# A transformer block on one core: the table of times is carried on through the second output product into the MLP, 81 pieces are shifted singly, and ScalarE makes both copies of the turned attention weights

## The chip, the cores and the metric

One core of one Trainium2 chip runs the whole kernel. The core has four engines that work at the same time, each through its own queue in order: TensorE (PE, matmuls), VectorE (DVE), ScalarE (ACT) and GpSimd (POOL); SyncE (SP) only issues DMAs, and ScalarE and GpSimd issue some too. The metric is the device time of one execution in microseconds (us); of several, the median is given. TensorE's clock can be granted in full or in half, and the profile shows which.

## The reference

One layer of a hybrid block for a sequence of 1024 tokens of 1024 features, float32 in and out. One half of the heads is a bidirectional matrix memory (mLSTM), the other half is differential attention; their outputs are concatenated, go through `w_out`, and an MLP with a squared ReLU follows. Cut to what matters:

```python
h = rms(x, norm1_g)
p = h @ w_in                                       # 1024 -> D_IN
qk_m  = silu(dwconv_centred(p[..., :1024], conv_w, conv_b))
mix_a = mlstm_group(qk_m, v, o, gates, ...)        # 4 heads x 128, chunks of 128, forward + backward
# differential attention, 4 heads, for each 128-query block:
logits = einsum('bmhqd,bmhkd->bmhqk', q, k) + bias # m = 0, 1
s   = softmax(logits, axis=-1)
a   = s[:, 0] - lam * s[:, 1]
o   = rms(a @ v, sub_g) * (1 - lam_init)
x = x + concat(mix_a, mix_b) @ w_out
u = rms(x, norm2_g) @ w_ff1                        # 1024 -> 4096
x = x + square(relu(u)) @ w_ff2                    # 4096 -> 1024
```

## The kernel before

Every large product is made with three matmuls: each float32 operand is cut into a high part (rounded, written by ScalarE) and a low part (operand less high part, by VectorE or GpSimd), and `mm3` (lines 157 to 160) sums high·high, high·low (line 159) and low·high (line 160) in PSUM. Tokens are handled in two halves of 512. The work goes in stages.

- **Projections and mLSTM** (to about 370 us). The order is written out by hand: pieces are pushed with a due time by `when` (line 280) into a heap, and `tick` runs the pieces that are due. ScalarE turns and normalises rows of a projection (`head_turn`: matmuls pzTrue on line 334, the scaling, the remainder on line 342), VectorE does a five-tap convolution (`conv`: the add into `pad` on line 646, taps on line 650, silu on 652), `keys` turns the keys (pk, line 705), and for each head `squares` and `unit` (root nd on line 89, scaling `to` on line 799, by GpSimd) feed the transposes po (line 805). Weights' low parts are cut by GpSimd on line 603 (`lo_c`, `lo_va`).
- **Attention** (370 to 605). 32 items (half, head, 128-query block). Per item: logits pl on PE (line 945), bias and row minimum on VectorE (950), exponentials on ScalarE (956), weights on VectorE (962 to 965), eight transposes into two PSUM tiles `pa` (972), the copies `at` out of them (977 by VectorE for the first four, 979 by ScalarE for the others), the product with the values in `pav` (986, one PSUM buffer), its squares by ScalarE (992), a root on GpSimd (89), the scaling `on` by VectorE (1001). After four items of a head a turn `pt` (1008, the same PSUM buffer as `pav`), and its high and low part `mix` (1013, 1017). The pieces of all items have due times from a table `A` and run in the order of time. In the first 12 items or so the products of the mLSTM's output gate stand between them on PE, and from item 18 on the products of `w_out` for the first half of the tokens; items 12 to 17 have neither.
- **Second half of `w_out`, norm and start of the MLP** (605 to 663). The table ends after item 31. From there the order is that of the code: `out_product(1)` (lines 1029 to 1072) is a generator that makes for each of 8 output blocks the cut of its weights (`split`, lines 133 and 134), its 24 matmuls pw, the add of x (1064), the square and its sum (1069, 1070); between its steps stand the root of the norm (`row_norms`: sums pr, root rc on line 89, transposes pb on 1084), the scalings of y (`normed`, 1328) and the cuts into high and low parts for the MLP (1293, 1296).
- **MLP** (663 to the end). A second table with its own `when` sorts the pieces: 7 products for each block (a Strassen-like scheme: sums of the four x blocks x1 to x7 against sums of weight blocks wa, wb, wd, we), whose intermediate sums v, w and sq VectorE forms from PSUM (1455, 1459, 1464), some of them through DRAM stores `g_dram`, then the second layer z.

All engines' queues follow these tables: a piece issues its instructions on its engine when its time comes in the order, and a load that a piece needs is issued on SP at the place of its own piece.

Of the kernel before, what the change touches and what calls it, by code (L numbers as in the profile page):

```python
# [48 lines left out]
def hybrid_block_kernel(ctx: ExitStack, tc: tile.TileContext, xT, w_v, w_kg, w_c, w_va, w_qa, w_o, w_1, w_2, vec, rel, onehot, outT):  # L49
# [924 lines left out]
    def att_copy(it, j2):  # L974
        it.ats[j2] = at = tpool.tile([P, HB], F32, tag="at", name=f"at{it.qb}{it.h}{j2}", bufs=4)
        if j2 == 0:
            nc.vector.tensor_copy(at, it.pa[j2])
        else:
            nc.scalar.activation(at, it.pa[j2], AF.Copy)
# [47 lines left out]
    r2, acc, rooted = {}, {}, {}  # L1027

    def out_product(half, psum):
        sl = slice(half * HB, (half + 1) * HB)  # L1030
        acc[half] = opool.tile([P, HB], F32, tag="yacc", name=f"yacc{half}")
        order = (4, 5, 6, 0, 1, 2, 3, 7)
        ps, ws = {}, {}

        def load(n):
            if n < KT:
                ws[n] = split(opool, w_o[n], "wo", opool, 3, 2, nc.vector, f"wo{half}{n}")

        def part(n, first, end):
            if first == 0:  # L1040
                load(n)
                ps[n] = psum(n)
            (whi, wlo), p = ws[n], ps[n]
            for j in range(first, end):
                k = order[j]
                kt = slice(k * P, (k + 1) * P)
                mm3(p, whi[:, kt], wlo[:, kt], mix[half][k][:, 0], mix[half][k][:, 1], j == 0, j == KT - 1)


        part(0, 0, KT - 1)  # L1050
        part(1, 0, KT // 2)
        yield
        part(1, KT // 2, KT - 1)
        for n in range(KT):
            if n < 2:
                part(n, KT - 1, KT)
            else:
                part(n, 0, KT // 2)
                yield
                part(n, KT // 2, KT)  # L1060
            p = ps[n]
            yt = y[half][n]
            nc.sync.dma_start(yt, xT[n][:, sl])
            nc.vector.tensor_tensor(yt, p, yt, op=ALU.add)
            if n == 0:
                nc.scalar.activation(acc[half], yt, AF.Square)
            else:
                sq = opool.tile([P, HB], F32, tag="ysq", name=f"ysq{half}{n}", bufs=1)
                nc.scalar.activation(sq, yt, AF.Square)
                nc.vector.tensor_tensor(acc[half], acc[half], sq, op=ALU.add)  # L1070
            nc.scalar.dma_start(y_dram[half][n], yt)
            yield
# [107 lines left out]
    def w_out(n):  # L1180
        raw = opool.tile([P, 1024], F32, tag="raw", name=f"raw_wo0{n}", bufs=2)
        hi = opool.tile([P, 1024], F32R, tag="woh", name=f"hi_wo0{n}", bufs=3)
        return hi, opool.tile([P, 1024], F32R, tag="wol", name=f"lo_wo0{n}", bufs=3), raw
# [80 lines left out]
    work = out_product(1, psum1)  # L1264
    next(work)
    att_turn(items[28:32], last)
    att_hi(items[31], last)
    att_lo(items[31], last)
# [596 lines left out]
```

## Time and profile before

| | us |
|---|---|
| median of 3 runs (lowest, highest) | 1292.5 (1292.22, 1293.47) |
| the profiled execution: time, span | 1292.14, 1290.4 |
| PE busy | 1257.0 |
| VectorE busy | 860.0 |
| ScalarE busy | 603.5 |
| GpSimd busy | 272.6 |
| mean granted TensorE clock | 0.993 |

The span is the profiled execution from its first to its last instruction; 1.7 us lie around it. A row of the profile's groups or timeline names line, engine, operation, the tile written and those read. In a timeline a row begins with the start and the duration, and in brackets stands how long the engine was idle before it and what it waited for. In the view of waits a row names the waiting group, the group waited for, the total, the number of times and the longest. Durations of neighbouring instructions of one engine overlap a little (VectorE's 0.69 us for 512 columns takes 0.60 of its queue, 1.22 us for 1024 columns takes 1.13).

### The profile page before, as it was taken

How to read it: one execution, taken by the hardware profiler on the slowest of the kernel's cores; microseconds unless marked ns; L12 is line 12 of the kernel's file. 1: busy time of each engine (PE TensorE's matmuls, PEld its weight loads, DVE VectorE, ACT ScalarE, POOL GpSimd, SP SyncE). 2: the span in 40 equal slices, each digit the busy share in tenths (PEclk: the TensorE clock that was granted, in tenths of full speed). 3: DMA queues.
4: the chain of work that ended last, by engine and by line, in shares of the span. 5: the costliest groups of instructions: out<-in, count | busy, mean ns of one | idle time of the engine just before them, and what ended most of it. 6: DMA issues, size and time to landing. Idle time of an engine off the chain costs nothing.

```text
span 1290.4 us, 17143 instructions
## 1 busy us (share of the span) xinstructions
PE 1257.0 (97%) x6443; PEld 1038.3 (80%) x6443; DVE 860.0 (67%) x1159; ACT 603.5 (47%) x1033; POOL 272.6 (21%) x273
## 2 busy tenths in 40 slices
PE   8999999999999989999999999999999999999998
PEld 6898678887878877888777788888887888888887
DVE  8635547886338888786748887666664675458754
ACT  5323336676535565563526554454444343333332
POOL 6623312554234344332000000000000000004001
PEclk9999999999999999999989999999999999999999
DMA  6415054544165475526524574454439946344732
GB/s 201 135 54 175 24 190 108 123 123 147 72 201 195 146 263 189 177 98 214 179 95 158 188 244 163 148 163 131 154 118 330 328 163 212 116 145 148 236 114 90
DMA packets 101459, 208.32 MB, mean 161 GB/s; under 512 B 8688, under 2 KB 21744, under 8 KB 101376
## 3 DMA queue, kind: packets, MB, share of 16 engines
q1 hardware_dynamic: 78368, 154.50, 37.6%
q10 hardware_dynamic: 15008, 31.50, 6.5%
q0 software_dynamic: 8000, 21.24, 5.0%
q8 instruction: 50, 0.82, 0.3%
q14 instruction: 33, 0.27, 0.1%
HBM read 148.90 MB, written 58.29 MB: 161 GB/s over the span
## 4 chain that ended last, share of the span: by engine, by line
PE 83%; DVE 8%; DMA 3%; issue 2%; ACT 2%; POOL 1%; SPq 0%; DVEq 0%; ACTq 0%; POOLq 0%
PE z L1707 8%; PE z L1705 8%; PE z L1706 8%; PE m L1376 7%; PE m L1377 7%; PE m L1378 7%; PE pav L986 4%; PE pl L945 3%; PE pv L235 3%; PE pw L158 2%; PE pa L972 2%; PE pw L160 2%; PE pw L159 2%; PE pj_c L158 2%; PE pj_c L159 2%
## 5 line engine op out<-in xcount | busy, mean ns | idle before, releaser
L1743 POOL TENSOR_TENSOR zx<-zx,res 128x512 f32<-128x512 f32 x4 | 8.7, 2180 | 503.8 <-DVE zx L1741 503.8
L1707 PE MATMUL z<-wbh,wa0l 128*128 128x512 f32 x224 | 87.4, 390 | 0.6 <-DVE wa0l L1296 0.6
L1705 PE MATMUL z<-wbh,wa0h 128*128 128x512 f32 x224 | 87.2, 389 | 0.0
L1706 PE MATMUL z<-wbl,wa0h 128*128 128x512 f32 x224 | 87.2, 389 | 0.0
L1706 PE MATMUL z<-wel,wa1h 128*128 128x512 f32 x224 | 87.1, 389 | 0.0
L1705 PE MATMUL z<-weh,wa1h 128*128 128x512 f32 x224 | 87.1, 389 | 0.0
L1707 PE MATMUL z<-weh,wa1l 128*128 128x512 f32 x224 | 87.1, 389 | 0.0
L950 DVE CUSTOM_DVE_ANT_0 l<-pl,toe 128x1024 f32<-128x1024 f32 x64 | 76.3, 1221 | 15.5 <-PE pl L945 14.4
L956 ACT ACTIVATE l<-l,sm 128x1024 f32<-128x1024 f32 x64 | 72.9, 1141 | 1.3 <-DVE sm L950 1.3
L1296 DVE TENSOR_TENSOR wel<-g,weh 128x1024 fp32r<-128x1024 f32 x28 | 35.2, 1258 | 56.5 <-ACT weh L1293 56.5
L1425 ACT ACTIVATE sq<-sq 128x512 f32<-128x512 f32 x48 | 30.3, 632 | 90.6 <-DVE sq L1464 69.0
L1296 DVE TENSOR_TENSOR wbl<-g,wbh 128x1024 fp32r<-128x1024 f32 x28 | 35.4, 1265 | 55.9 <-ACT wbh L1293 55.9
L1293 ACT ACTIVATE weh<-g 128x1024 fp32r<-128x1024 f32 x28 | 29.7, 1060 | 90.2 <-PE z L1707 53.4
L1293 ACT ACTIVATE wbh<-g 128x1024 fp32r<-128x1024 f32 x28 | 29.7, 1061 | 89.9 <-PE z L1707 52.6
L986 PEld LDWEIGHTS pav<-v,at 128*128 128x128 f32 x512 | 62.9, 195 | 9.3 <-DVE on L1001 4.6
L986 PE MATMUL pav<-v,at 128*128 128x128 f32 x512 | 64.4, 280 | 4.5 <-DVE on L1001 2.9
L160 PE MATMUL pw<-mix,lo_wo 128*128 128x512 f32 x128 | 51.5, 402 | 4.2 <-DVE lo_wo L134 4.2
L158 PE MATMUL pj_c<-hhi,hi_c 128*128 128x512 f32 x128 | 53.5, 418 | 0.0
L945 PE MATMUL pl<-kk,q 64*128 64x512 f32 x384 | 53.3, 408 | 0.0
L158 PE MATMUL pw<-mix,hi_wo 128*128 128x512 f32 x128 | 53.2, 415 | 0.0
L159 PE MATMUL pw<-mix,hi_wo 128*128 128x512 f32 x128 | 51.1, 399 | 0.0
L159 PE MATMUL pj_c<-hlo,hi_c 128*128 128x512 f32 x128 | 50.7, 396 | 0.0
(459 smaller groups left out, 3680.2 us busy)
## 6 DMA issues: line engine op xcount, KB each, us to landing
g<-g_dram SPq DMA_DIRECT2D x56, 512.0 KB, 4.1
g_dram<-gs SPq DMA_DIRECT2D x64, 256.0 KB, 4.3
g_dram<-sq ACTq DMA_DIRECT2D x42, 256.0 KB, 2.2
kk<-k_dram POOLq DMA_DIRECT2D x16, 512.0 KB, 5.6
raw_wo<-in_w_o_dram SPq DMA_DIRECT2D x16, 512.0 KB, 4.7
re<-in_w_dram SPq DMA_DIRECT2D x16, 512.0 KB, 4.4
ro<-in_w_dram SPq DMA_DIRECT2D x16, 512.0 KB, 3.7
zt<-in_w_dram SPq DMA_DIRECT2D x16, 512.0 KB, 4.1
```

The costliest lines, as they stand in the source:

```text
L158: nc.tensor.matmul(out, ahi, bhi, start=start, stop=False)
L159: nc.tensor.matmul(out, ahi, blo, start=False, stop=False)
L160: latest[0] = nc.tensor.matmul(out, alo, bhi, start=False, stop=stop).ins
L945: nc.tensor.matmul(it.pl[x][:, sl], hd.q[r, i, qi * P : (qi + 1) * P], hd.kk[r, j, sl], start=n == 0, stop=n == 2)
L950: nc.vector.tensor_tensor_reduce(lt, it.pl[m], hd.toe[:, off : off + S], 1.0, 3.0e38, ALU.add, ALU.min, it.sm[:, m : m + 1])
L986: nc.tensor.matmul(it.pav[:, 0:P], at, it.head.v[:, c], start=c == 0, stop=c == NC - 1)
L1376: nc.tensor.matmul(p, wh, xh, start=go, stop=False, skip_group_check=True)
L1377: nc.tensor.matmul(p, wh, xl, start=False, stop=False, skip_group_check=True)
L1378: nc.tensor.matmul(p, wl, xh, start=False, stop=stop and k == 3, skip_group_check=True)
L1705: nc.tensor.matmul(p, wh, gh, start=go, stop=False, skip_group_check=True)
L1706: nc.tensor.matmul(p, wh, gl, start=False, stop=False, skip_group_check=True)
L1707: nc.tensor.matmul(p, wl, gh, start=False, stop=end, skip_group_check=True)
```

## The change

Three things.

1. Two tables of numbers `moved`: 55 pieces of the first heap (numbered in the order in which they are pushed) and 26 of the MLP's table get their due time shifted singly. Number 36 is the transposes of the 14th block of pzTrue, number 25 the high part of the fourth `va` weights, numbers 92 and 95 the `unit` of the mLSTM's first head's first half and a `squares` piece after it.
2. `att_copy`: both copies are made by ScalarE; VectorE has 32 instructions fewer, ScalarE 32 more.
3. The second output product is no longer a generator. Its steps (load, high, low, two or three groups of matmuls, load of x, add, square, sum), the last head's turn, the norm, the scalings and cuts for the MLP and the loads and cuts of its first weights become pieces of the same heap with due times of their own; the heap runs on to the end of this stage. The PE, GpSimd and SP queues keep their number of instructions.

```diff
+    moved = {
+        20: 0.16, 25: -2.784, 36: 2.075, 37: 0.745, 43: -0.133, 92: 2.944, 95: 2.082, 122: -0.259, 124: 2.027,
...
     def when(t, f, *args):
-        heapq.heappush(table, (t, len(made), f, args))
+        heapq.heappush(table, (t + moved.get(len(made), 0.0), len(made), f, args))
         made.append(t)
...
     def att_copy(it, j2):
         it.ats[j2] = at = tpool.tile([P, HB], F32, tag="at", name=f"at{it.qb}{it.h}{j2}", bufs=4)
-        if j2 == 0:
-            nc.vector.tensor_copy(at, it.pa[j2])
-        else:
-            nc.scalar.activation(at, it.pa[j2], AF.Copy)
+        nc.scalar.activation(at, it.pa[j2], AF.Copy)
...
-    def out_product(half, psum):
...
-        floor = A["SW"] + 0.01 if pre == "O" else -99.0
+        floor = max(floor, A["SW"] + 0.01 if pre in "OH" else -99.0)
...
-    while table:
-        t, _, f, args = heapq.heappop(table)
-        f(*args)
-    order.close()
-    load_mix(1)
+    def h_part(V, n, first, end):
+        if first == 0:
+            V[0] = psum1(n)
+        k_order = (4, 5, 6, 0, 1, 2, 3, 7)
+        hi, lo, _ = V["w"][0]
+        for j in range(first, end):
+            k = k_order[j]
+            kt = slice(k * P, (k + 1) * P)
+            mm3(V[0], hi[:, kt], lo[:, kt], mix[1][k][:, 0], mix[1][k][:, 1], j == 0, j == KT - 1)
...
+    for n in range(KT):
+        t = A["HF"] + u * parts_at[n][0][0]
+        V = {"w": split_ahead(lambda n=n: w_out(n, 1), w_o[n], nc.vector, t, "H", room_at(n))}
+        for p, first, end in parts_at[n]:
+            when(A["HF"] + u * p, h_part, V, n, first, end)
+        t = A["HF"] + u * ends[n]
+        when(max(t + A["HX"], A["S2"] + 0.02), h_room, n)
+        when(t + A["HE"], h_add, V, n)
+        when(t + A["HQ"], h_square, V, n)
+        when(t + A["HA"], h_sum, V, n)
...
-    for n, _ in enumerate(work):
-        if n == 2:
-            next(norms, None)
-        if 3 <= n < 7:
-            j = n - 3
-            normed(0, j)
-            cut(*x_part(1 + j // 2, block(j // 2, 0), j % 2))
-        if 6 <= n < 10:
-            with tc.issue_after(rooted[0]):
-                cut(w_a(n - 6), raw_e[n - 6])
-            if n < 8:
-                load_e(n - 4)
+    when(A["N0"], next, norms)
+    when(A["N1"], next, norms, None)
+    for j in range(4):
+        t = A["XN"] + j * A["XD"]
+        when(t, normed, 0, j)
+        when(t + A["XH"], lambda a: cut_hi(*a), x_part(1 + j // 2, block(j // 2, 0), j % 2))
+        when(t + A["XL"], lambda a: cut_lo(*a), x_part(1 + j // 2, block(j // 2, 0), j % 2))
+        t = A["WN"] + j * A["WD"]
+        when(A["RE"] if j < 2 else t - 2 * A["WD"] + A["WL"] + 0.01, load_e, j)
+        when(t, lambda c: cut_hi(w_a(c), raw_e[c]), j)
+        when(t + A["WL"], lambda c: cut_lo(w_a(c), raw_e[c]), j)
+    run(1e9)
+    order.close()
...
     def when(t, f, *args):
-        table.append((t, len(table), f, args))
+        table.append((t + moved.get(len(table), 0.0), len(table), f, args))
```

How this moves instructions, at three places. First ScalarE around items 12 to 15 of the attention (`l` are score tiles, their rows the exponentials; `on` the squares of a product; `pa` the turned weights; the digits of a name are query block, head and part). Before:

```order
L956 ACTIVATE l231_4314,sm23_4296<-l231_4314,sm23_4296 128x1024
L992 ACTIVATE on03_4420,sm03_4178<-pav03_4408 128x128
L979 ACTIVATE at131_4438<-pa131_4433 128x512
L148 ACTIVATE hi_wo00_4402<-raw_wo00_4401 128x1024
L956 ACTIVATE l330_4366,sm33_4351<-l330_4366,sm33_4351 128x1024
L956 ACTIVATE l331_4405,sm33_4351<-l331_4405,sm33_4351 128x1024
L992 ACTIVATE on13_4479,sm13_4232<-pav13_4467 128x128
```

and now:

```order
L966 ACTIVATE l231_4314,sm23_4296<-l231_4314,sm23_4296 128x1024
L986 ACTIVATE at131_4421<-pa131_4408 128x512
L999 ACTIVATE on03_4432,sm03_4178<-pav03_4423 128x128
L148 ACTIVATE hi_wo00_4402<-raw_wo00_4401 128x1024
L986 ACTIVATE at130_4439<-pa130_4416 128x512
L966 ACTIVATE l330_4367,sm33_4352<-l330_4367,sm33_4352 128x1024
L966 ACTIVATE l331_4405,sm33_4352<-l331_4405,sm33_4352 128x1024
L999 ACTIVATE on13_4479,sm13_4244<-pav13_4467 128x128
```

The copy at130, on VectorE before, stands in ScalarE's queue behind a weight cut; the copy at131 moves ahead of the squares of the item before.

Second, VectorE in the second output product, from the sixth block's low part to the seventh's (lo_wo15 and lo_wo16; r20 is the norm's factor, x1l and x2l the low parts for the MLP, wa0l that of its first weights). Before:

```order
L134 TENSOR_TENSOR lo_wo15_5987<-raw_wo15_5985,hi_wo15_5986 128x1024
...
L1328 SCALAR_TENSOR_TENSOR y0_0_4382<-y0_0_4382,cst_185,r20_5889 128x512 x2
L1328 SCALAR_TENSOR_TENSOR y0_1_4383<-y0_1_4383,cst_185,r20_5889 128x512 x2
L1296 TENSOR_TENSOR x1l_5791<-y0_0_4382,x1h_5790 128x1024
L1064 TENSOR_TENSOR y1_1_5787<-pw13_5897,y1_1_5787 128x512
L1296 TENSOR_TENSOR x1l_5791<-y0_1_4383,x1h_5790 128x1024
...
L1296 TENSOR_TENSOR x2l_5793<-y0_2_4384,x2h_5792 128x1024
L1064 TENSOR_TENSOR y1_2_5788<-pw14_5942,y1_2_5788 128x512
L1296 TENSOR_TENSOR x2l_5793<-y0_3_4385,x2h_5792 128x1024
L1070 TENSOR_TENSOR yacc1_5721<-yacc1_5721,ysq14_5973 128x512
L134 TENSOR_TENSOR lo_wo16_6030<-raw_wo16_6028,hi_wo16_6029 128x1024
```

and now:

```order
L1076 TENSOR_TENSOR lo_wo15_5908<-raw_wo15_5906,hi_wo15_5907 128x1024
L1243 TENSOR_TENSOR yacc1_5863<-yacc1_5863,ysq13_5971 128x512
L1304 TENSOR_TENSOR wa0l_5798<-re0_5828,wa0h_5797 128x1024
L1336 SCALAR_TENSOR_TENSOR y0_1_4383<-y0_1_4383,cst_185,r20_5917 128x512 x2
L1336 SCALAR_TENSOR_TENSOR y0_2_4384<-y0_2_4384,cst_185,r20_5917 128x512 x2
L1232 TENSOR_TENSOR y1_2_5791<-pw14_5939,y1_2_5791 128x512
L1304 TENSOR_TENSOR x1l_5794<-y0_0_4382,x1h_5793 128x1024
L1076 TENSOR_TENSOR lo_wo16_5954<-raw_wo16_5952,hi_wo16_5953 128x1024
```

Of the four cuts x1l and x2l that stood ahead of lo_wo16 three now stand behind it, and of the eight scalings between the two low parts four are left; the cut wa0l has come in.

Third, VectorE at the start of the MLP (ro0 and re0b are weight blocks and sums of them, the x are parts of the activations, v and w intermediate sums). Before:

```order
L1296 TENSOR_TENSOR x6l_6111<-y1_3_5789,x6h_6110 128x1024
L1296 TENSOR_TENSOR wd0l_5803<-ro0_6135,wd0h_5802 128x512
...
L1518 TENSOR_TENSOR re0b_6241<-re0b_6241,ro0_6135 128x512
L1296 TENSOR_TENSOR wbl_5799<-re0b_6241,wbh_5798 128x512
...
L1296 TENSOR_TENSOR x7l_6115<-y1_0_5786,x7h_6114 128x1024
L1455 TENSOR_TENSOR v_0_6414<-m0_1_6376,x1_b0_6344 128x512
L1296 TENSOR_TENSOR x7l_6115<-y1_1_5787,x7h_6114 128x1024
```

and now:

```order
L1304 TENSOR_TENSOR wd0l_5806<-ro0_6135,wd0h_5805 128x512
...
L1529 TENSOR_TENSOR re0b_6241<-re0b_6241,ro0_6135 128x512
L1304 TENSOR_TENSOR x6l_6111<-y1_3_5792,x6h_6110 128x1024
...
L1304 TENSOR_TENSOR x7l_6115<-y1_0_5789,x7h_6114 128x1024
L1304 TENSOR_TENSOR x7l_6115<-y1_1_5790,x7h_6114 128x1024
L1466 TENSOR_TENSOR v_0_6418<-m0_1_6376,x1_b0_6343 128x512
```

The sums into re0b stand ahead of the second x6l cut, and both x7l cuts ahead of v.

In the mLSTM stage the four transposes of the 14th block of pzTrue stand on PE 12 matmuls later, behind the last of pj_c4; on GpSimd the root nd00 and the scaling to00 stand behind the selects e11 and the low part lo_c3, and not ahead of them; the high part hi_va3 stands earlier on ScalarE.

More of the change, by code (lines that the diff above doesn't have):

```diff
@@ L1025, in load_mix @@
             nc.gpsimd.dma_start(mix[half][h], mx_dram[h][half])
-    r2, acc, rooted = {}, {}, {}
-    def out_product(half, psum):
[L1030 to L1072, printed above, removed]
+    r2, acc = {}, {}
     def row_norms(half):
@@ L1079, in row_norms @@
         nc.vector.tensor_scalar(rc, pc[:, 0:4], D * EPS, None, op0=ALU.add)
-        rooted[half] = rsqrt(rc, rc, 4).ins
+        rsqrt(rc, rc, 4)
         yield
@@ L1178, in hybrid_block_kernel, with w_out @@
     ypool = yq = y = cctx = opool = None
[L1180 to L1183, printed above, removed]
+    def w_out(n, half=0):
+        raw = opool.tile([P, 1024], F32, tag="raw", name=f"raw_wo{half}{n}", bufs=2)
+        hi = opool.tile([P, 1024], F32R, tag="woh", name=f"hi_wo{half}{n}", bufs=3)
+        return hi, opool.tile([P, 1024], F32R, tag="wol", name=f"lo_wo{half}{n}", bufs=3), raw
     def first_half():
@@ L1240, in item_pieces @@
         on("ON", att_unit)
-        if n % 4 == 3 and n < 31:
+        if n % 4 == 3:
             V = {}
@@ L1251, in hybrid_block_kernel, with h_room, h_add, h_square @@
         item_pieces(n, it)
-    last = {}
-    while table:
-        t, _, f, args = heapq.heappop(table)
-        f(*args)
-    order.close()
-    load_mix(1)
+    def h_part(V, n, first, end):
[7 more added lines that the diff above has]
+            mm3(V[0], hi[:, kt], lo[:, kt], mix[1][k][:, 0], mix[1][k][:, 1], j == 0, j == KT - 1)
+    def h_room(n):
+        nc.sync.dma_start(y[1][n], xT[n][:, HB:])
+    def h_add(V, n):
+        nc.vector.tensor_tensor(y[1][n], V[0], y[1][n], op=ALU.add)
+    def h_square(V, n):
+        if n == 0:
+            acc[1] = opool.tile([P, HB], F32, tag="yacc1", name="yacc1")
+        V["sq"] = acc[1] if n == 0 else opool.tile([P, HB], F32, tag="ysq", name=f"ysq1{n}", bufs=1)
+        nc.scalar.activation(V["sq"], y[1][n], AF.Square)
+        nc.scalar.dma_start(y_dram[1][n], y[1][n])
+    def h_sum(V, n):
+        if n > 0:
+            nc.vector.tensor_tensor(acc[1], acc[1], V["sq"], op=ALU.add)
     def psum1(n):
@@ L1262, in psum1, with room_at, run @@
         return psF.tile([P, HB], F32, tag=f"q{4 + n % 4}", name=f"pw1{n}")
[L1264 to L1268, printed above, removed]
+    when(A["LM"], load_mix, 1)
+    u = A["HS"]
+    parts_at = {0: ((0, 0, 7), (3.5, 7, 8)), 1: ((1.75, 0, 4), (2.75, 4, 7), (3.75, 7, 8))}
+    ends = {0: 3.75, 1: 4.0}
+    for n in range(2, KT):
+        parts_at[n] = ((2 * n, 0, 4), (2 * n + 1, 4, 8))
+        ends[n] = 2 * n + 2.0
+    def room_at(n):
+        return A["HF"] + u * ends[n - 3] + 0.01 if n > 2 else -99.0
+    for n in range(KT):
[8 more added lines that the diff above has]
+        when(t + A["HA"], h_sum, V, n)
+    def run(until):
+        while table and table[0][0] < until:
+            _, _, f, args = heapq.heappop(table)
+            f(*args)
+    run(A["S2"])
     bctx.close()
@@ L1334, in x_part @@
         return xf[i], src[j], (slice(None), slice(2 * j, 2 * j + 2))
-    load_e(0)
-    load_e(1)
-    next(work)
     psctx.close()
@@ L1360, in hybrid_block_kernel @@
     order.enter_context(tc.manual_schedule())
+    moved = {
[3 rows of a table added]
+    }
     table = []
     def when(t, f, *args):
-        table.append((t, len(table), f, args))
+        table.append((t + moved.get(len(table), 0.0), len(table), f, args))
     bank = {}
```

10 lines of the change are left out of this document (6 added, 4 removed), and 9 rows, old and new, of the table moved.

## The prediction

> **What bounds the kernel now.** I read the page's totals first, then TensorE's waits, then windows around each wait, then timelines of the engine named there.
>
> ```profile
> span 1290.4 us, 17143 instructions
> PE 1257.0 (97%) x6443; PEld 1038.3 (80%) x6443; DVE 860.0 (67%) x1159; ACT 603.5 (47%) x1033; POOL 272.6 (21%) x273
> ```
>
> TensorE is busy for 1257.0 of 1290.4 us and its matmuls are not touched, so all that can be won is its 33.4 us of idle time and the time that it runs at half clock. The waits name the owners:
>
> ```profile
> PE pw L160 <- DVE lo_wo L134: 4.2, 1, 4.2
> PE pav L986 <- DVE on L1001: 2.9, 3, 1.5
> PE pva L159 <- POOL lo_va L603: 2.6, 2, 1.6
> PE m L1376 <- DVE sq L1464: 2.4, 1, 2.4
> PE pav L986 <- DVE mix L1017: 1.6, 1, 1.6
> PE pb L1084 <- POOL rc L89: 1.4, 1, 1.4
> PE pt L1008 <- DVE on L1001: 1.2, 2, 0.6
> PE m L1377 <- DVE x7l L1296: 0.8, 2, 0.5
> PE pk L705 <- ACT k L148: 0.4, 1, 0.4
> ```
>
> (Microseconds, times, longest.) Most belong to VectorE, although it works only 67% of the span: it is late in a few places. Windows show those places and what a wait does to the clock (after the window: its length, then PE, PEld, DVE, ACT, POOL busy, PEclk, DMA, GB/s):
>
> ```profile
> 452.74:489.62 36.88, 31.87 (x246) 27.00 (x244) 31.99 (x59) 22.38 (x48) 19.58 (x34) 0.95 0.76 251
> 489.62:579.25 89.63, 89.63 (x601) 74.41 (x601) 71.49 (x125) 52.66 (x103) 32.27 (x50) 1.00 0.47 154
> 190.19:193.22 3.03, 3.03 (x15) 2.44 (x13) 2.93 (x4) 0.60 (x1) 0.00 (x0) 1.00 0.68 243
> 294.80:298.21 3.41, 1.79 (x8) 1.19 (x7) 3.30 (x6) 2.64 (x4) 2.20 (x2) 1.00 0.03 7
> 298.21:301.63 3.42, 2.40 (x15) 1.87 (x14) 3.35 (x4) 0.00 (x0) 2.33 (x1) 1.00 0.51 161
> 472.30:475.71 3.41, 1.27 (x11) 0.78 (x8) 3.17 (x6) 2.31 (x5) 1.63 (x4) 1.00 0.99 348
> 475.71:479.13 3.42, 3.42 (x19) 3.42 (x18) 2.36 (x5) 0.26 (x2) 0.00 (x0) 0.50 1.11 401
> 646.38:653.21 6.83, 5.58 (x13) 4.44 (x14) 3.62 (x5) 0.63 (x1) 0.00 (x0) 0.50 0.10 38
> 707.82:711.23 3.41, 1.01 (x5) 0.56 (x4) 3.41 (x5) 0.88 (x1) 0.00 (x0) 1.00 0.00 0
> 711.23:714.65 3.42, 3.42 (x9) 2.65 (x9) 2.98 (x5) 2.93 (x6) 0.00 (x0) 0.50 0.21 79
> ```
>
> The window at 190.19 holds 13 matmul starts (two of its 15 reach in from before): 0.23 us for one of 512 columns at full clock. A stretch of 3.41 us with 1.62 us of PE idle (294.80) is followed by full clock, stretches with 2.14 us (472.30) and 2.40 us (707.82) by half clock. A wait so costs its length and, above a limit between 1.6 and 2.1 us, another 1.71 us (half of 3.41). The Trainium skill, TensorE: Matmul & The Clock Gate, section "Why this matters for your kernels", asks only that no PE gap exceed about 3 us, one idle window of some 3.4 us bringing the half clock back; the two rows above contradict it, and I go by the rows.
>
> **The change part by part.**
>
> *Attention, items 12 to 17 (452.74 to 489.62).* Here no other products stand between the items. PE is idle 5.01 us and one stretch runs at half clock, so 6.72 us is the most to win; the next window, with fillers, has PE 100% busy and nothing to win from copies.
>
> ```profile
> L977 DVE COPY at<-pa x32: 680/688/693, 390.4 to 603.8; 128x512 f32<-128x512 f32 x32
> L979 ACT ACTIVATE at<-pa x32: 589/599/602, 389.4 to 604.3; 128x512 f32<-128x512 f32 x32
> 461.03 0.68 DVE L977 COPY at<-pa 128x512 f32<-128x512 f32 x1
> 461.63 0.34 DVE L1001 TENSOR_SCALAR on<-pav,sm 128x128 f32<-128x128 f32 x1
> ```
>
> VectorE's copy holds its queue 0.60 us (461.03 to 461.63), right ahead of the `on` for which the next product waits. Seven items free 4.2 us of a VectorE that is busy 31.99 of 36.88; ScalarE takes seven copies of 0.60 and goes from 22.38 to 26.6, below PE's 31.87. Neither is then the bound, but the two copies of an item run one behind the other, so a product's second half can start up to 0.60 later. Following the waits item by item, about 2.1 us of idle are left, none of it 2 us in one stretch: 2.9 of idle and 1.7 of clock, **−4.6** (0 if ScalarE's order takes everything back, −6.7 if all waits go). In the other 26 items the extra 0.60 us lies behind gate and w_out products on PE: I take 0; uncovered it is rival A.
>
> *The wait of 0.6 before a turn (pt, near 587).*
>
> ```profile
> L134 DVE TENSOR_TENSOR lo_wo<-raw_wo,hi_wo x8: 1215/1224/3165, 578.5 to 647.5; 128x1024 fp32r<-128x1024 f32 x8
> ```
>
> The first lo half of the second output product (3.17 us, 578.5) stands on VectorE ahead of that turn and leaves; **−0.6** (0 to −0.6).
>
> *Output product of the second half (605 to 663).* Two waits. The transposes pb now stand half a product behind the sums pr, and not beside them: 12 matmuls of 0.23 are 2.8 us, over the POOL root that PE waits 1.4 for.
>
> ```profile
> 631.59 1.22 DVE L134 TENSOR_TENSOR lo_wo<-raw_wo,hi_wo 128x1024 fp32r<-128x1024 f32 x1
> 634.05 2.74 DVE L1328 SCALAR_TENSOR_TENSOR y<-y,cst,r 128x512 f32<-128x512 f32 x4
> 646.35 2.36 DVE L134 TENSOR_TENSOR lo_wo<-raw_wo,hi_wo 128x1024 fp32r<-128x1024 f32 x2
> 647.63 0.80 PE L160 MATMUL pw<-mix,lo_wo 128*128 128x512 f32 x1 [4.18 <-DVE lo_wo L134]
> raw_wo<-in_w_o_dram SPq DMA_DIRECT2D x16, 512.0 KB, 4.7
> ```
>
> The root goes from exposed to covered: **−1.4** (0 to −1.4). For the large wait, lo_wo16 starts 14.8 us behind lo_wo15 (631.59 to 646.35). In the new VectorE order only this stands between them, with the rows' durations: lo_wo15 1.22, a sum 0.69, wa0l 1.22, four scalings 2.74, an add 0.69, the first x1l 1.22, together 7.8 us. So it would end at 640.6 or earlier; PE asks for it at 643.45 (647.63 less 4.18), 642.0 with the root's wait gone: 1.4 us to spare. The wait goes (−4.18) and with it 5.58 us of running at half clock (−2.79): **−7.0**. SP's loads are re-ordered too: raw_wo16 is issued once lo_wo14 has freed its buffer, some 8 us ahead of its cut, against 4.7 to landing. Bounds: −7.0, and −2.0 if the load comes its 4.7 us later and about 3.3 of it is exposed with its clock.
>
> *Start of the MLP (699 to 715).*
>
> ```profile
> 690.24 1.23 DVE L1296 TENSOR_TENSOR x6l<-y,x6h 128x1024 fp32r<-128x1024 f32 x1 [1.38 <-ACT x6h L1293]
> 694.28 0.63 ACT L1293 ACTIVATE wbh<-re0b 128x512 fp32r<-128x512 f32 x1 [1.70 <-DVE re0b L1518]
> 702.55 0.69 DVE L1455 TENSOR_TENSOR v<-m,x_b 128x512 f32<-128x512 f32 x1 [0.38 <-DMA g_dram<-v_s]
> 710.23 0.68 DVE L1464 TENSOR_TENSOR sq<-w,m 128x512 f32<-128x512 f32 x1
> ```
>
> Four 512-wide operations up to the re0b sum now stand ahead of the second x6l cut (690.24) and use the 1.38 us for which VectorE idled there. The sum so ends 2.5 earlier (1.38 and the cut's 1.13). ScalarE's wbh waited 1.70 for it; it starts 1.7 earlier, and with it v_s and its store, for which v waits: v at 700.8 and not 702.55. Between v and sq one x7l cut (1.22 with overlap 1.13) leaves and a wbl cut (0.6) enters. So sq comes some 2.2 to 2.5 earlier; the x7l waits (0.8) and a shorter one for wel go because those cuts precede v. Stage: **−2.5** in length. PE then arrives earlier too, so the wait for sq shrinks from 2.40 to about 1.6 only, the length that left the clock alone at 294.80: **−1.7** for the clock, the term I am least sure of. Bounds: 0, if the store lands as late as before, and −5.8, if the wait for sq goes too.
>
> By the skill's 3 us neither this wait nor that of 472.30 could have cost a half clock, and taking both away would win 2 × 1.71 less: the sum would be −12.4 in place of −15.8.
>
> *mLSTM stage: three single shifts that reach the path.*
>
> ```profile
> 190.10 0.69 ACT L148 ACTIVATE zzTrue<-pzTrue,cst 128x512 fp32r<-128x512 f32 x1 [1.19 <-PE pzTrue L334]
> 192.87 1.23 DVE L646 TENSOR_TENSOR pad<-pj_c,rb 128x1024 f32<-128x1024 f32 x1
> 249.38 3.38 POOL L603 TENSOR_TENSOR lo_c<-raw_c,hi_c 128x1024 fp32r<-128x1024 f32 x1
> 254.59 0.60 PE L805 MATMUL po<-ident,to 128*128 128x128 f32 x4
> 298.18 2.36 POOL L603 TENSOR_TENSOR lo_va<-raw_va,hi_va 128x1024 fp32r<-128x1024 f32 x1 [1.21 <-ACT hi_va L148]
> ```
>
> The transposes of pzTrue13 go 12 matmuls (2.8 us) back. ScalarE's row of 190.10 moves to 192.9 and the VectorE remainder behind it ends near 194.3, in VectorE's queue ahead of the pad add of 192.87; that add, the taps that hang on it and, behind them, the silu and the pk transposes, which already wait 0.4 for ScalarE, come 1.45 later: **+1.45** (0 if the taps take it up). On GpSimd the scaling of `to00` goes behind lo_c (249.38 + 3.38, done at 252.7), so it ends near 255.5, and PE asks at 254.59: **+1.3** for it with the hand-over (0 to 1.4). hi_va3 goes 2.8 us earlier on ScalarE, lo_va3 then starts as lo_va2 ends, near 297.0 and not 298.18: of the second pva wait **−0.7** (0 to −1.0). The other shifts move work inside idle time: 0. Stage: **+2.05**.
>
> *Sum.* 2.05 − 4.6 − 0.6 − 1.4 − 7.0 − 2.5 − 1.7 = −15.8. The profiled execution took 1292.14, 0.36 under the median of 1292.5; I predict from the median: **1276.7 us**.
>
> **The rivals.**
>
> *A, slower: ScalarE's queue stalls every product.* The `at0` copy now stands in ScalarE's order behind 1.14 us exponentials and ahead of at1. If each of the 32 items paid x, 15.8/32 = 0.49 us is where nothing is left; with a whole copy, 0.60, it is 19.2 − 15.8 = +3.4: 1296. Against it: PE is 100% busy from 489.62 to 579.25 with ScalarE at 52.66 of 89.63 and at1 standing behind the same exponentials. The Trainium skill, TensorEngine Tiling (Array Packing), section "PSUM Bottleneck", advises both ScalarE and VectorE for emptying PSUM, which speaks against this part of the change; this trace speaks for the change as long as VectorE is the late one of the two.
>
> *B, the tail keeps a wait:* a load or cut of the second output product comes late and the clock falls again: +5.0 on the forecast (its bound): 1281.7. For it: SP runs in order and gets the weights of the MLP between.
>
> *C, the attention wins nothing:* the waits of items 12 to 17 pass from VectorE to ScalarE: +4.6, 1281.3. For it: ScalarE's copies of 0.60 one behind the other; against it, its 22.38 of 36.88.
>
> *D, the mLSTM shifts cost nothing*: VectorE takes up the 1.45 in the idle time ahead of the silu, GpSimd's lo_c ends nearer to the 2.36 us of the like operation at 298.18: −2.75, 1274.0. Against it: the pk wait of 0.4 says that this chain had nothing left to give.
>
> *E, no change:* the gains come back as new waits at each place (fillers moved earlier are missing later): 1290 to 1295, around 1292.
>
> **How the numbers follow.** Forecast .54 (its own range 1275 to 1279.5: the upper end with the MLP's half clock kept, +1.7, and 1 us lost elsewhere), D .14, C .12, B .10, E .05, A .05. About 2.6 us (0.2%) can be told from no change. Faster is the first four, .90; same .05; slower .05. For 8 in 10 the range takes in the forecast, D and most of B and C: 1272.5 to 1283.5.
>
> **What would show it.** The wait for lo_wo gone and no half clock between 630 and 650; the wait for sq near 1.6 and no half clock behind it; between 450 and 490 PE idle near 2 us, ScalarE with 64 copies of 0.60; pk waiting near 1.9, po near 1.3. Wrong it is if pav shows waits for ScalarE in items with fillers (A), if lo_wo or raw_wo appears under the waits (B), or if idle time around items 12 to 17 stays at 5 us (C).

## The result, and the profile after

The changed kernel takes 1272.54 us (median of 4 runs, 1271.97 to 1272.84) beside 1292.36 for the kernel before, ratio 0.9845 with a 95% interval of 0.9828 to 0.9862. Timed again beside later kernels it was 1271.81 against 1292.31, ratio 0.9847 (0.9831 to 0.9862). So it is 1.55% faster: about 20 us, where 15.8 were forecast. The first median lies 0.04 us above the low end of the range given, 1272.5, the second 0.7 below it.

The totals and the chain on the page of the changed kernel:

```profile
span 1270.7 us, 17176 instructions
PE 1249.3 (98%) x6443; PEld 1034.0 (81%) x6443; DVE 836.2 (66%) x1127; ACT 617.7 (49%) x1065; POOL 270.6 (21%) x273
PE 84%; DVE 6%; DMA 3%; ACT 3%; POOL 2%; issue 2%; SPq 0%; ACTq 0%; POOLq 0%; DVEq 0%
```

PE's busy time fell by 7.7 us with the same 6443 matmuls: most of that is time at half clock that is gone (four stretches, 13.66 us, half of which is 6.8). The rest of the 19.7 us of span is idle time. TensorE's waits, in the form shown before (us in total, times, longest; rows of stages that the change leaves alone are left out):

```profile
PE pk L715 <- ACT k L148: 1.7, 1, 1.7
PE pav L993 <- DVE on L1008: 1.5, 1, 1.5
PE m L1387 <- DVE sq L1475: 1.5, 2, 1.3
PE pav L993 <- DVE mix L1024: 0.7, 1, 0.7
PE pt L1015 <- DVE on L1008: 0.4, 1, 0.4
PE pav L993 <- ACT at L986: 0.4, 1, 0.4
PE pva L159 <- POOL lo_va L613: 0.3, 1, 0.3
```

The waits for lo_wo, for the root rc, for x7l and wel are gone; pk waits longer, as forecast; the two waits for lo_va, 2.6 in all, are down to 0.3, where only 0.7 of them was forecast to go.

To see where the time went I cut both traces at the same instructions (the first matmuls of pzTrue, pk, po, the last of pva with lo_va, the logits of items 12 and 20, the last logits, the first matmuls of the MLP's x1, x6 and x4 products, of z, and the end) and read the windows between. Of before, then of after (window, length, PE, PEld, DVE, ACT, POOL busy, PEclk, DMA, GB/s):

```profile
175.77:204.28 28.51, 26.49 (x130) 20.83 (x128) 20.83 (x19) 12.13 (x14) 4.77 (x3) 1.00 0.74 218
204.28:254.59 50.31, 50.31 (x294) 43.80 (x295) 40.05 (x51) 36.33 (x102) 20.33 (x16) 1.00 0.38 89
254.59:361.03 106.44, 103.54 (x611) 89.15 (x609) 67.62 (x96) 65.33 (x183) 48.53 (x37) 1.00 0.37 118
455.33:504.45 49.12, 44.11 (x321) 36.95 (x321) 41.86 (x76) 29.87 (x62) 22.72 (x37) 0.97 0.70 235
584.89:660.79 75.90, 69.64 (x354) 58.03 (x353) 47.01 (x65) 30.12 (x46) 9.93 (x18) 0.96 0.48 165
695.30:711.05 15.75, 12.17 (x49) 8.55 (x48) 14.64 (x18) 5.95 (x9) 0.00 (x0) 1.00 0.54 168
711.05:980.40 269.35, 269.35 (x1153) 217.02 (x1154) 185.43 (x266) 127.75 (x194) 0.00 (x0) 0.99 0.51 174
```

```profile
175.25:205.00 29.75, 26.45 (x130) 20.82 (x128) 21.64 (x19) 12.12 (x14) 5.47 (x3) 1.00 0.62 202
205.00:255.59 50.59, 50.48 (x294) 43.76 (x294) 39.49 (x52) 36.60 (x103) 18.70 (x16) 1.00 0.40 100
255.59:359.33 103.74, 103.07 (x609) 89.36 (x610) 66.94 (x96) 65.29 (x182) 47.96 (x37) 1.00 0.42 117
453.63:499.28 45.65, 42.55 (x321) 35.51 (x320) 37.30 (x68) 33.26 (x70) 24.03 (x38) 1.00 0.76 253
579.72:645.85 66.13, 66.13 (x353) 56.30 (x353) 41.84 (x58) 31.18 (x50) 8.21 (x18) 1.00 0.56 195
680.36:692.99 12.63, 11.37 (x50) 8.82 (x48) 12.29 (x16) 4.62 (x7) 0.00 (x0) 1.00 0.66 203
692.99:961.13 268.14, 267.95 (x1152) 215.78 (x1153) 185.69 (x266) 127.73 (x195) 0.00 (x0) 1.00 0.51 173
```

| stretch | forecast | measured |
|---|---|---|
| to the first pzTrue | 0 | -0.52 |
| pzTrue to pk (pzTrue13 later) | +1.45 | +1.24 |
| pk to po (to00 later) | +1.3 | +0.28 |
| po to the last lo_va matmul (hi_va3 earlier) | -0.7 | -2.70 |
| attention, items 12 to 20 | -4.6 | -3.47 |
| second output product, with the turn | -9.0 | -9.77 |
| MLP, x6 to x4 products | -2.5 | -3.12 |
| MLP, x4 to z (its half clock) | -1.7 | -1.21 |
| from z to the end | 0 | -0.38 |
| sum | -15.8 | -19.65 |

The stretches not listed are equal to 0.01 us. In words: the three mLSTM stretches together were forecast at +2.05 and came out at -1.18. That 3.2 us is most of the 3.9 that are missing.

### The profile page after: what moved, and what is told of

It is laid out like the page before. It is cut to its first block, busy times and chain, and to the rows that moved or that the text cites. A ratio compares the mean times of both kernels' runs of the same rounds, so it can differ in the third digit from the quotient of the medians.

```text
span 1270.7 us, 17176 instructions
## 1 busy us (share of the span) xinstructions
PE 1249.3 (98%) x6443; PEld 1034.0 (81%) x6443; DVE 836.2 (66%) x1127; ACT 617.7 (49%) x1065; POOL 270.6 (21%) x273
## 4 chain that ended last, share of the span: by engine, by line
PE 84%; DVE 6%; DMA 3%; ACT 3%; POOL 2%; issue 2%; SPq 0%; ACTq 0%; POOLq 0%; DVEq 0%
PE z L1718 8%; PE z L1717 8%; PE z L1716 8%; PE m L1387 7%; PE m L1388 7%; PE m L1389 7%; PE pav L993 4%; PE pl L955 4%; PE pv L235 3%; PE pw L158 2%; PE pw L160 2%; PE pw L159 2%; PE pa L982 2%; PE po L158 1%; PE po L160 1%
## 5 line engine op out<-in xcount | busy, mean ns | idle before, releaser
L960 DVE CUSTOM_DVE_ANT_0 l<-pl,toe 128x1024 f32<-128x1024 f32 x64 | 76.3, 1221 | 16.9 <-PE pl L955 15.8
L158 PE MATMUL pw<-mix,hi_wo 128*128 128x512 f32 x128 | 52.3, 408 | 0.0
L160 PE MATMUL pj_c<-hhi,lo_c 128*128 128x512 f32 x128 | 50.5, 394 | 0.0
```

Source lines behind the costliest of these rows:

```text
L158: nc.tensor.matmul(out, ahi, bhi, start=start, stop=False)
L160: latest[0] = nc.tensor.matmul(out, alo, bhi, start=False, stop=stop).ins
L960: nc.vector.tensor_tensor_reduce(lt, it.pl[m], hd.toe[:, off : off + S], 1.0, 3.0e38, ALU.add, ALU.min, it.sm[:, m : m + 1])
```

## The experiments

Three theories stood for the mLSTM stage. *Additive*: each delay is carried to the end, as in the prediction. *Absorbing*: delays ahead are taken up by the lo_va waits behind. Later a third, *two outcomes*: a race between VectorE and GpSimd decides which wait the stage shows. For the other stages the question was which part of the change made the gain. Below, "the stage" is the time from the first pzTrue to the last matmul with lo_va: 185.26 us in the first profile of before, 184.08 in that of the changed kernel.

### One shift taken out: number 36 (pzTrue13)

```diff
-        20: 0.16, 25: -2.784, 36: 2.075, 37: 0.745,
+        20: 0.16, 25: -2.784, 37: 0.745,
```

> The changed kernel with only the shift of number 36 taken out, so that the transposes of pzTrue13 stand 12 matmuls earlier again. Additive theory (as in the prediction: each delay in the mLSTM stage is carried to the end): the wait of pk shrinks from 1.7 to 0.4 us and the time from 1272.5 to 1271.3. Absorbing theory (behind pk the matmuls of pva wait for GpSimd's lo_va2 and lo_va3, whose chain does not hang on pk, so that PE's earlier arrival is waited away there): pk waits 0.4 again, the waits for lo_va grow by about 1.2 in return, and the time stays within 0.4 of 1272.5.

Measured: 1270.97, ratio to before 0.9831 (0.9816 to 0.9846). The pk wait fell to 0.25, the lo_va waits rose from 0.3 to 1.05, and the stage took 183.62, only 0.46 less than with the shift. The stretch up to pk is 1.41 shorter (28.34 for 29.75). So the delay is real where it arises, and two thirds of it are taken up behind. The timing points to 1.5 us less than the changed kernel, which the intervals don't tell from 0.5.

### One shift taken out: number 25 (hi_va3)

```diff
-        20: 0.16, 25: -2.784, 36: 2.075,
+        20: 0.16, 36: 2.075,
```

> The changed kernel with only the shift of number 25 taken out: hi_va3 stands on ScalarE where it stood before, later. Prediction's price: 0.7 us lost, 1273.2. Absorbing theory with lo_va3 as what sets the end of the stage: lo_va3 starts 1.5 to 2.5 us later, so the wait for it grows from 0.3 to about 2 us: 1274.0 to 1274.8.

Measured: 1278.41, ratio 0.989 (0.9872 to 0.9908), stage 191.29. Both theories miss: the shift is worth 7.2 us of stage, not 0.7 and not 2. The waits in the window from 290 to 305 us:

```profile
PE pva L159 <- POOL lo_va L613: 2.9, 1, 2.9
PE pva L158 <- ACT hi_va L148: 2.0, 1, 2.0
```

The second wait is new. It is not for the low part that I had looked at, but for the high part that ScalarE makes. Half clock follows for two stretches (6.83 us), and lo_va3, the cut made from this high part, itself took 3.29 us.

### All 24 shifts of the mLSTM stage taken out

```diff
-        heapq.heappush(table, (t + moved.get(len(made), 0.0), len(made), f, args))
+        heapq.heappush(table, (t + (moved.get(len(made), 0.0) if len(made) > 300 else 0.0), len(made), f, args))
```

> The changed kernel without the 24 shifts with numbers below 300 (all in the mLSTM stage); attention, second output product and MLP as changed. Additive theory: the stage gets back its 2.05 us, 1270.5. Absorbing theory, by the trace of the changed kernel (stage 1.2 us shorter than before): 1273.7, with the two lo_va waits of 1.6 and 1.0 back and pk at 0.4.

Measured: 1275.46, ratio 0.9863 (0.9841 to 0.9884), stage 188.11. The direction is that of the absorbing theory, but the waits are not the expected ones: 1.9 for hi_va, 1.95 for lo_va, with half clock. This kernel has the same order of instructions in this stage as before on every engine, yet the stage is 2.85 longer than in the first profile of before. One profile of before had not shown what this order usually does.

### The kernel before, profiled again

No edit.

> The kernel before, unchanged, for a second profiled execution. Theory of two outcomes (the mLSTM stage from the first pzTrue to the last lo_va matmul takes 185.3 us where GpSimd loses a race for lo_va1 against VectorE, as in the first profile, and 188.1 where it wins, as in two kernels with the same order in this stage): the stage takes 188.1, with a wait for hi_va of 1.9 and a half clock behind it, and GpSimd's lo_va1 takes 2.4 and not 3.4 us. Rival, that the first profile shows the usual execution: 185.3, waits of 1.6 and 1.0 for lo_va.

Measured: 1292.02, ratio 1.000 (0.999 to 1.001); the profiled execution 1295.16; stage 187.93. The window of the stage in the first profile:

```profile
175.77:361.03 185.26, 180.33 (x1032) 153.78 (x1030) 128.50 (x165) 113.79 (x298) 73.64 (x55) 1.00 0.43 125
```

and in the second, with the two stretches in which PE waits for hi_va and lo_va and then runs at half clock:

```profile
175.16:363.09 187.93, 181.76 (x1032) 155.02 (x1030) 128.74 (x165) 113.69 (x298) 73.15 (x55) 0.99 0.43 124
297.46:300.87 3.41, 0.50 (x1) 0.19 (x1) 3.30 (x5) 1.26 (x2) 2.07 (x1) 1.00 0.00 0
300.87:304.28 3.41, 3.06 (x10) 2.48 (x10) 3.38 (x3) 0.00 (x0) 0.30 (x1) 0.50 0.51 156
```

The same program does this stage in 185.3 or in 187.9 us. What differs stands in the timelines (start, duration, engine, line, operation). First profile: VectorE's small operation on nd and its product qs, GpSimd's lo_va1, VectorE's next product qs, GpSimd's lo_va2, ScalarE's scaling of k:

```profile
286.74 0.54 DVE L797 TENSOR_SCALAR nd<-nd 128x4 f32<-128x4 f32 x1
287.12 1.21 DVE L756 TENSOR_TENSOR qs<-q,qs 128x1024 f32<-128x1024 f32 x1
287.20 3.38 POOL L603 TENSOR_TENSOR lo_va<-raw_va,hi_va 128x1024 fp32r<-128x1024 f32 x1
292.99 1.76 DVE L756 TENSOR_TENSOR qs<-q,qs 128x1024 f32<-128x1024 f32 x1
293.62 3.35 POOL L603 TENSOR_TENSOR lo_va<-raw_va,hi_va 128x1024 fp32r<-128x1024 f32 x1
295.92 1.24 ACT L148 ACTIVATE k<-pad,vecs 128x1024 f32<-128x1024 f32 x1 [0.66 <-DVE pad L646]
```

Second profile:

```profile
286.04 2.39 POOL L603 TENSOR_TENSOR lo_va<-raw_va,hi_va 128x1024 fp32r<-128x1024 f32 x1
286.16 2.30 DVE L797 TENSOR_SCALAR nd<-nd 128x4 f32<-128x4 f32 x1
288.37 1.21 DVE L756 TENSOR_TENSOR qs<-q,qs 128x1024 f32<-128x1024 f32 x1
291.91 2.38 POOL L603 TENSOR_TENSOR lo_va<-raw_va,hi_va 128x1024 fp32r<-128x1024 f32 x1
292.36 3.01 DVE L756 TENSOR_TENSOR qs<-q,qs 128x1024 f32<-128x1024 f32 x1
296.54 1.24 ACT L148 ACTIVATE k<-pad,vecs 128x1024 f32<-128x1024 f32 x1 [1.86 <-DVE pad L646]
297.68 1.04 ACT L148 ACTIVATE hi_va<-raw_va 128x1024 fp32r<-128x1024 f32 x1
```

Whoever begins first delays the other, and the two meet twice. At the first meeting qs began 0.08 us ahead of lo_va1 in the first profile, and lo_va1 took 3.38 us. In the second lo_va1 began 0.12 ahead of the operation on four columns, which then took 2.30 us and ended when lo_va1 did, at 288.4. This alone does not make VectorE late: counted from the first pzTrue, it begins its next product qs at 117.22 in the first profile and at 117.20 in the second. But GpSimd, not held up, begins lo_va2 at 116.75 instead of 117.85. So at the second meeting the order is turned round too: in the first profile qs begins 0.63 ahead of lo_va2 and takes 1.76, in the second lo_va2 begins 0.45 ahead and qs takes 3.01. From there VectorE is 1.2 us late with the pad add, ScalarE with the scaling of k that waits for it, and hi_va3, which stands behind that scaling in ScalarE's queue, makes PE wait. The cut lo_va3 ends 1.24 us later (126.01 instead of 124.77, counted the same way), and the half clock adds 1.4.

The Trainium skill, SBUF — State Buffer, section "SBUF: two separate sides", says that VectorE and GpSimd share one pair of ports, an exclusive lock that the first to start holds for its whole instruction while the other is fully blocked; on VectorE's side this holds for operations in a two-port mode or with two SBUF inputs. The rows agree for qs, which reads two SBUF tiles: it took 3.01 us and ended 1.08 after lo_va2. The 2.30 us of the small operation, which reads one, agree if it runs in such a mode, which no run here shows.

### One more instruction on GpSimd in the kernel before

```diff
-            for d in range(2):
+            for d in (0, 1, 1) if (h, g) == (2, 1) else (0, 1):
                 ...
                 nc.gpsimd.affine_select(
```

> The kernel before with one more instruction on GpSimd: the second affine select ahead of lo_va1 is made twice (it only repeats a masking that is already there), so lo_va1 begins 1.1 to 1.5 us later. Theory of the race: VectorE's small operation on nd (held 2.3 us by lo_va1 in the second profile of before) and the qs product get through first, lo_va1 takes 3.4 in place of 2.4 us, the pad add and the k scaling come earlier, the wait for hi_va shrinks from 1.9 to under 0.5, and the stage from the first pzTrue to the last lo_va matmul takes 185 to 186.5 us: more work on GpSimd, about 2 us less in all, 1289.5 to 1291. Rival, GpSimd's chain is itself what the end of the stage hangs on: stage 188 to 189.5, 1292.3 to 1294.

Measured: 1290.88 against 1293.06, ratio 0.9988 (0.9977 to 1.0); the profiled execution 1288.48; stage 185.63. The timeline at the same place:

```profile
283.60 0.59 DVE L797 TENSOR_SCALAR nd<-nd 128x4 f32<-128x4 f32 x1
284.10 1.21 DVE L756 TENSOR_TENSOR qs<-q,qs 128x1024 f32<-128x1024 f32 x1
284.18 3.39 POOL L603 TENSOR_TENSOR lo_va<-raw_va,hi_va 128x1024 fp32r<-128x1024 f32 x1
```

GpSimd was given more to do and the stage became 2.30 us shorter than in the second profile of before, as the theory of the race asks and the rival excludes: the small operation gets through, lo_va1 takes 3.39, no wait for hi_va is left. The waits are 1.7 and 1.0 for lo_va, near the 1.6 and 1.0 of the first profile, and the stage is within 0.4 us of its 185.26. The timing agrees with the theory but hardly tells the gain from none (0.12%, the interval ends at 1.0). The runs of before lay between 1288.2 and 1295.2 in the largest group, 24 of them. That would fit a mixture of both outcomes, but only two of its executions were profiled.

### The mLSTM shifts alone, and number 25 alone, in the kernel before

```diff
-        heapq.heappush(table, (t, len(made), f, args))
+        heapq.heappush(table, (t + moved.get(len(made), 0.0), len(made), f, args))
```

with the 24 numbers of this stage in `moved`:

> The kernel before with only the 24 shifts of the mLSTM stage. Additive theory (prediction): +2.05, 1294.5. Absorbing theory, by the stage's lengths in the two traces: -1.2, 1291.2, with the lo_va waits at 0.3 and the pk wait at 1.7.

Measured: 1289.19 against 1292.17, ratio 0.9973 (0.9964 to 0.9983); stage 184.10. It is 3 us less, where the stage is 1.16 shorter than in the first profile of before and 3.83 shorter than in the second. This fits executions of before that are mostly worse in this stage than its first profile, but doesn't show it. The additive sum misses in sign, the absorbing theory's 1291.2 by 2 us. With only `25: -2.784`:

> The kernel before with only the shift of number 25 (hi_va3 2.8 us earlier on ScalarE). Additive theory: the shift is worth as much here as its removal cost the changed kernel (stage 7 us longer): 1285 to 1286. Theory that its worth depends on who is late besides it: here only the second lo_va wait of 1.0 can shrink, 1291.5 to 1292.5.

Measured: 1288.44, ratio 0.9966 (0.9954 to 0.9978); stage 182.68. Both expectations miss in between. It is 2.6 us shorter than the first profile of before and 5.25 shorter than the second. Like for like is the second: lo_va1 took 2.39 there as here. With hi_va3 ahead of the scaling of k, the late scaling no longer reaches PE. The other outcome of the race was not seen with hi_va3 ahead. The other 23 shifts make the stage 1.42 us longer (184.10 less 182.68).

### The changed kernel, and the same with only number 25 of the mLSTM shifts

> The changed kernel, unchanged, beside the others of this call: 1272.5; stage 184.1 as in its first profile under every theory, since hi_va3 no longer stands behind the work that the race delays.

Measured: 1271.81, stage 184.11, as in the first profile.

```diff
-        ... (t + moved.get(len(made), 0.0), ...
+        ... (t + (moved.get(len(made), 0.0) if len(made) in (25,) or len(made) > 300 else 0.0), ...
```

> The changed kernel with, of the 24 shifts in the mLSTM stage, only number 25 (hi_va3) kept. Theory that number 25 makes the whole gain of the stage and the other 23 cost about 1.4 us (by the stage lengths of the kernels that have them alone and together): 1271.1. Theory that the others are needed with it: 1272.5 or more.

Measured: 1270.17 (1269.27 to 1270.61), ratio 0.9831 (0.9817 to 0.9844), stage 182.72, span 1268.4 beside 1270.4. The stage is 1.39 shorter than in the changed kernel, the time 1.6 less; the intervals of the two ratios overlap, but the stage lengths repeat: 184.08, 184.11 and 184.10 with all 24 shifts, 182.68 and 182.72 with number 25 alone. By its median this is the fastest of the kernels.

### The first copy back on VectorE

```diff
+        if j2 == 0:
+            nc.vector.tensor_copy(at, it.pa[j2])
+        else:
+            nc.scalar.activation(at, it.pa[j2], AF.Copy)
-        nc.scalar.activation(at, it.pa[j2], AF.Copy)
```

> The changed kernel with the first copy of each item on VectorE again, all due times as changed. Theory that VectorE's copy was the late work of items 12 to 17: those items lose the 3.5 us that the change won there, 1276.0, with a half clock back if idle time of 2 us falls into one stretch. Rival, that the shifted due times did it and the engine of the copy is indifferent: within 0.5 of 1272.5. Rival, that the items with fillers profit too: over 1277.

Measured: 1276.32, ratio 0.9874 (0.9859 to 0.9889): 3.7 us of time lost by the ratios. Between items 12 and 20 the kernel gains 0.2 us over before instead of 3.47. Of these 3.27, 1.49 are idle time (4.59 instead of 3.10) and the rest is a half clock that is back. The waits from 450 to 490 us name the copy:

```profile
PE pav L996 <- DVE at L987: 3.8, 4, 2.1
PE pav L996 <- DVE mix L1027: 0.7, 1, 0.7
```

### The copies alone in the kernel before

The same edit the other way round, in the kernel before.

> The kernel before with one edit: both copies of an item on ScalarE; no due time shifted, everything else as before. Theory that VectorE's copy is the late work of items 12 to 17 and of the turn near 587: 3.5 to 4.6 us less than before, 1288 to 1289. Rival, that the gain needs the shifted due times as well: 1291.5 to 1293. Rival A of the prediction (each product waits for ScalarE): over 1294.

Measured: 1289.74 against 1292.17, ratio 0.9979 (0.9968 to 0.999). Between the logits of items 12 and 20:

```profile
454.61:501.54 46.93, 42.37 (x322) 35.25 (x322) 37.46 (x68) 33.20 (x70) 24.92 (x37) 1.00 0.74 247
```

That is 2.4 us in the timing, less than the first theory expected and more than the second. The stretch is 2.19 shorter than the 49.12 of before, but only 0.45 of this is idle time (4.56 instead of 5.01); the rest is a half clock that did not come. It can stay away without the copies: the kernel with the mLSTM shifts alone has the order of before from attention on, and in its profile the stretch has the idle time of before, 4.98, and no half clock:

```profile
453.03:500.51 47.48, 42.50 (x321) 35.36 (x320) 41.75 (x76) 29.85 (x62) 22.89 (x38) 1.00 0.74 246
```

So the idle time tells what the edits do: 5.01 before, 4.56 with the copies alone, 4.59 with the due times alone (the experiment above), 3.10 with both. Most of it needs both. The half clock came in four of the five profiles with this order of before, in none of the seven with both edits; how often it comes with the copies alone is not shown. The due times here include one that the list of changes does not name: that of the turn's low part, `TL` in the table `A`, went from 4.151 to 4.177.

### The MLP's 26 shifts taken out

```diff
-        table.append((t + moved.get(len(table), 0.0), len(table), f, args))
+        table.append((t, len(table), f, args))
```

> The changed kernel without the 26 shifts of the MLP's table. Prediction's price for them: 2.5 of waits and 1.7 of clock, so 1276.7 with the wait for sq at 2.4 and a half clock behind it. Rival, that the start of the MLP gained because the stage ahead of it was reordered: within 1 us of 1272.5.

Measured: 1276.02, ratio 0.9882 (0.9867 to 0.9896): 4.8 us by the ratios, against 4.2 forecast. The waits of before are back (0.34, 0.29, 2.40 for sq), and one of 0.81 behind them, but no half clock followed in the profiled execution. So the agreement with 4.2 is partly luck: the 1.7 in it for the clock was not lost there. The wait of 2.40 was cut in two by the border of two stretches of 3.41 us (counted back from the half-clock stretch at the end of the record):

```profile
689.11:692.52 3.41, 2.16 (x10) 1.40 (x8) 3.38 (x5) 0.71 (x1) 0.00 (x0) 1.00 0.11 41
692.52:695.94 3.42, 2.28 (x10) 1.78 (x11) 3.35 (x5) 2.50 (x4) 0.00 (x0) 1.00 0.00 0
695.94:699.35 3.41, 3.41 (x16) 2.57 (x15) 2.79 (x5) 3.35 (x6) 0.00 (x0) 1.00 0.20 77
```

With the first copy back on VectorE a wait of 1.85 fell into one stretch, and half clock did follow:

```profile
690.84:694.25 3.41, 1.56 (x8) 0.96 (x7) 3.38 (x6) 1.27 (x2) 0.00 (x0) 1.00 0.48 189
694.25:697.66 3.41, 3.41 (x9) 2.65 (x10) 3.26 (x5) 2.89 (x5) 0.00 (x0) 0.50 0.21 77
```

## Why the prediction was right or wrong

The direction was right, and the likeliest story with its places held; the size was 4 us short, and the sum failed at one stage.

- **The step that failed: the mLSTM stage's "+2.05", in which "+1.45" and "+1.3" are carried to the end of the stage.** The end of this stage hangs on the end of lo_va3, for which PE waits last, and not on when PE arrives. In us from the first pzTrue, out of the timelines:

| kernel | lo_va3 ends | stage | between |
|---|---|---|---|
| before, first profile | 124.77 | 185.26 | 60.49 |
| before, second profile (one half-clock stretch) | 126.01 | 187.93 | 61.92 |
| before, one more instruction on GpSimd | 125.15 | 185.63 | 60.48 |
| changed | 123.59 | 184.08 | 60.49 |
| changed, number 36 taken out | 123.13 | 183.62 | 60.49 |
| changed, number 25 taken out (two half-clock stretches) | 128.32 | 191.29 | 62.97 |
| changed, of these shifts only number 25 | 122.24 | 182.72 | 60.48 |

  Up to po the two delays came to 1.24 and 0.28. They ended in what had been a wait of 1.6 for lo_va2, a row of the view that the prediction shows. What the stage gained, 1.18, is what lo_va3 ended earlier.
- **"Of the second pva wait -0.7":** I priced hi_va3 by the wait that stood in the one profile, a wait for GpSimd. In three of the four profiles with the order of before in this stage (the second of before and two kernels with other edits) PE waits here for hi_va3 itself, behind a scaling of k that VectorE makes late, and half clock follows. There the shift is worth 5.2 to 5.4 us of the stage, and taken out of the changed kernel it costs 7.2. In the outcome of the first profile it was not tried by itself. I had looked at what a piece is moved past on its own engine only for the two shifts that I priced as losses.
- **"+1.45" for pzTrue13:** right at pk (+1.24), wrong that it is carried to the end: two thirds come back as shorter lo_va waits. All 23 shifts other than number 25 cost 1.4 us together, and they cost it because lo_va3 ends that much later.
- **"+1.3" for to00:** it cost 0.28, and with pzTrue13 back the stretch is as long (50.58), so this does not hang on the other delay. In the changed kernel's trace lo_c3 took 2.42 us instead of 3.38:

```profile
249.41 2.42 POOL L613 TENSOR_TENSOR lo_c<-raw_c,hi_c 128x1024 fp32r<-128x1024 f32 x1
```

  The scaling ended at 255.54 and po began at 255.59 after a wait of 0.1; with a lo_c3 of 3.38 both would have come about 1 us later (an estimate from these two durations). Which of the two engines came first was not part of my count. That this is the cause is argued from the rows, not tested by itself.
- **Attention, -4.6:** -3.47. That VectorE's copy is late work is shown (with it back, PE waits 3.8 us for it); that the copies alone bring the gain is not: most of the idle time won needs the due times too. The term was a quarter too large: 3.1 us of idle time were left, not 2.1, the largest wait, 1.5, for `on`, just as before.
- **The turn and the second output product, -9.0:** -9.77. The 7.25 us between lo_wo15 and lo_wo16 compare with 7.8 counted, and the 1.4 us to spare are what the trace shows (632.15 + 1.22 against 634.75). Idle time fell by 6.26 as forecast; PE's busy time fell by 3.5 where the half clock had been priced at 2.8.
  The rows of VectorE's two low parts and PE's first matmul with the second, after:

```profile
624.90 1.22 DVE L1076 TENSOR_TENSOR lo_wo<-raw_wo,hi_wo 128x1024 fp32r<-128x1024 f32 x1
632.15 1.22 DVE L1076 TENSOR_TENSOR lo_wo<-raw_wo,hi_wo 128x1024 fp32r<-128x1024 f32 x1
634.75 0.39 PE L160 MATMUL pw<-mix,lo_wo 128*128 128x512 f32 x1
```

- **MLP, -2.5 and -1.7:** -3.12 and -1.21; the wait for sq became 1.26, shorter than the 1.6 expected, and the half clock is gone. Without the 26 shifts 4.8 us come back, so the gain is theirs and not that of the stage ahead.
- **To the first pzTrue, 0:** this stretch differs by up to 3.4 us between executions of kernels with the same code there (172.3 to 175.8 us); a half-clock stretch near 20 us goes with it: the eight profiles that have one reach pzTrue at 174.6 to 175.8 us, the six without at 172.3 to 173.5. The first profile of before was the slowest of all in this stretch, and the faster of the two of before in the mLSTM stage. The two hid each other in a total near the median.
- **The rivals:** A did not happen; PE waits once for a copy on ScalarE, for 0.4 us. B and C did not happen either. D had the nearest number (1274.0), and half of its cause came true: lo_c3 took 2.42 us, as D said, but VectorE did not take up the 1.45, of which 1.24 arrived at pk. The advice of the Trainium skill cited at A (TensorEngine Tiling (Array Packing), "PSUM Bottleneck") did not pay here: with the due times as changed, both copies on ScalarE left 3.10 us of idle time between items 12 and 20, one on each engine 4.59.

## What to carry to other kernels

A wait in one profile is one outcome of who came first: before pricing a move, see whether the stage looks the same in a second execution, above all where VectorE and GpSimd work at the same time. What an in-order queue is worth is read from what a piece is moved past (here a scaling that waits for another engine), not from the wait that happens to be visible. And losses ahead of a later wait are not additive with it: find the work that the last wait of a stage is for (here lo_va3), give the stage the change in its end, and add only across stages.

## What the runs showed of the hardware that was not expected

- VectorE and GpSimd can hold up each other's instructions. GpSimd's 128x1024 subtraction took 2.4 or 3.4 us, VectorE's operation on 128x4 took 0.54 or 2.30 and its product qs 1.76 or 3.01. The order at the first meeting, where the two began 0.08 and 0.12 us apart, went with a stage that ended 2.7 us earlier or later.
- The half clock depends on how a wait lies. Of the stretches of 3.41 us in the rows above, those in which PE was busy for 1.79 us or more kept full clock, and those with 1.56 or less lost it for the next stretch. Elsewhere in these traces 1.61 lost it (second profile of before, 474.95 to 478.36) and 1.66 kept it (all 24 mLSTM shifts out, 294.71 to 298.13), but 1.49 in the last stretch with matmuls kept it too (changed, only number 25, 1262.88 to 1266.30): about half a stretch, and not a sharp limit. A wait of 1.85 inside one stretch cost a half clock, one of 2.40 across a border did not. The Trainium skill's rule of no gap over about 3 us (TensorE: Matmul & The Clock Gate, "Why this matters for your kernels") is too generous by these rows.
